# A hybrid attention and RWKV-7 layer on one core: buffers of the NSA product, gates and two key pieces moved, the second triangular solve handed out in pairs of steps, and a TensorE residual add at the end

## The chip, the cores and the metric

The kernel runs on one core of one Trainium2 chip. The metric is the device time of one execution in microseconds; lower is better. The kernel before takes 563.45 us, the median of three runs (563.41 to 565.96). One more execution was recorded by the hardware profiler, and all rows shown here come from that one.

## What is computed

One decoder layer on 256 tokens of width 2048, all in float32. Both head groups read one projection of the normalised input:

```python
h = rms_norm(x, pre_norm_g)            # (256, 2048)
feat = h @ w_in                        # q, six K/V sets, 24 gates, z_A, z_B, and r, k, v, w, a of RWKV
A = nsa_mixer(q, kc, vc, ks, vs, kw, vw, gates, ...)   # 8 heads of 128, 2 K/V groups:
                                       # compressed + selected + sliding-window attention, gated
B = rwkv7_mixer(...)                   # 16 heads of 64, a recurrence over the 256 tokens
mix = concat([A * silu(z_A), B * silu(z_B)])
out = x + rms_norm(mix @ w_out, post_norm_g)
```

The recurrence of RWKV-7 is computed in four chunks of 64 tokens, which takes triangular 32 by 32 systems, solved by substitution.

## The kernel before, in words

**Products.** A float32 operand is split into a rounded part H and a rest L, and a product is the sum of H·xH, H·xL and L·xH, so that each weight piece costs TensorE three matmuls for each 128 rows. The input projection runs over 57 pieces of 128 output features, in this order: wa (piece 0), k/r/v of the first half of the RWKV heads (1 to 12), kc, kc, vc, vc, ks, ks, kw, kw (13 to 20), k/r/v of the second half (21 to 32), q (33 to 40), z_A (41 to 48), z_B (49 to 56); the V pieces and gates, computed token-major, come ahead of piece 37. Each piece has two halves of 8 K-tiles; the weights of piece j, half h are called `hfjh` and `lfjh` (`hf191`: H of piece 19, second half), those of the output product `ho`, `lo`. SP loads a half into one of four raw buffers, ScalarE makes H (L309), VectorE makes L (L310). TensorE adds a piece up in one of two PSUM buffers of `ppool`, and VectorE empties it in `evacuate` (L594, from piece 35 on L596 and L597). Before a piece can start, the piece two ahead of it must have been emptied.

**Beside the projection** stand generators that issue a few instructions and yield: the RWKV blocks, `solve(hb)` for each half of the heads, `compress` (with weights `cw` that SP loads into the arena, L1008), and eight `nsa_head`s. Small operands of attention and the chain go through PSUM buffers called `banks`. A Python planner with estimated due times picks which one goes on, and a scheduler of the Tile framework then sets the order of each engine's instructions. On the chip each engine runs its instructions strictly in that order, and a wait for one holds all that stand behind it.

**The solve.** `us` carries the systems from the tile GR over DRAM into the arena (L799, L805). Then 31 steps of two VectorE operations each (L812, L814) follow, and the generator yields after each step. A copy (L817), a round trip over DRAM in two orders (`zt`, L820 and L829; `zs`, L821 and L838), two rounds of 32-column matmuls, and a chain over four chunks come behind it. In each step of the chain TensorE multiplies VS by KT and GR (64 by 64), VectorE empties the results (L908, L925, L935), and the next step needs them.

**Buffers.** The arena has 51 units of 128 by 256 floats, handed out and given back in program order. `xs0` and `xs1` (tags X0 and X1) hold the split input. The product of attention and gate, `mixA`, is split into 16 tiles (hi and lo; L1190 on ScalarE, L1191 on VectorE) in X1's buffer, which is read until the last half of the projection, `hf560`/`lf560`. `ks` and `kw` are emptied into an arena unit, from which L1281 and L1282 make KCH and KCL. Each z piece takes an arena unit until it has been used.

**The end.** The output product runs in four column parts of 512, for two blocks i of 128 tokens. The last three weight groups of the fourth part are done for i = 0 first. Then `finish` takes the root mean square, multiplies by `post_norm_g` (L1374), scales and adds x (L1372 on VectorE, for 512 columns L1375 on ScalarE and L1376 on GpSimd), and stores.

## Time and profile before

| | us |
|---|---|
| median of three runs | 563.45 |
| the profiled execution, its own time | 563.78 |
| its span in the trace | 562.0 |
| TensorE busy in it | 543.9 |
| VectorE busy | 436.2 |
| ScalarE busy | 320.0 |
| GpSimd busy | 58.8 |

The span is what the trace covers; 1.78 us of the profiled execution's time lie outside it. TensorE's busy time says how much of the span its matmuls fill, not how fast they were: a matmul record's end is modelled, and a record that runs at half clock is twice as long. So idle time of TensorE and its granted clock have to be read together, and a wait is best measured from the start of one group of matmuls to the start of the next, against the same group elsewhere.

### The profile page before, as it was taken

Reading aid. Unit: us, or ns where it says so; the run is one execution under the profiler, and the core shown is the slowest. Engines: PE = TensorE matmul, PEld = TensorE weight load, DVE = VectorE, ACT = ScalarE, POOL = GpSimd, SP = SyncE. Lnnn points to the kernel's source line nnn. Section 1 sums busy time; section 2 is a strip of 40 time slices with the busy share of each in tenths; the row PEclk is TensorE's granted clock in tenths of the full one; section 3 lists DMA queues with packets and bytes.
Section 4 is the critical chain, followed back from the end, with each engine's and each line's share of the span. In section 5 each row is a group of like instructions: output and inputs, shape, how many; then the busy total and the mean of one; then the engine's idle time right before and its main releaser. Section 6 shows DMA issues by size and latency. Waiting matters only on the chain. (4 is left out here: it accounts for less than half of the span.)

```text
span 562.0 us, 11515 instructions
## 1 busy us (share of the span) xinstructions
PE 543.9 (97%) x4444; PEld 496.4 (88%) x4444; DVE 436.2 (78%) x911; ACT 320.0 (57%) x592; POOL 58.8 (10%) x95
## 2 busy tenths in 40 slices
PE   9999999998799999999999999999999989999994
PEld 9999999997799999998998888888888877888883
DVE  6878997974799977678699969998757556756655
ACT  6958854743235543446767677776654345745532
POOL 3201310420000000001306100100000010000002
PEclk9999999999699999999999999999999999999997
DMA  8957455477554585643445353444644435867624
GB/s 295 377 193 263 144 177 170 151 239 217 188 188 168 172 245 185 199 152 119 138 152 188 126 147 128 162 162 141 197 150 155 152 109 184 304 187 218 194 76 150
DMA packets 41459, 102.02 MB, mean 182 GB/s; under 512 B 14235, under 2 KB 16956, under 8 KB 40764
## 3 DMA queue, kind: packets, MB, share of 16 engines
q1 hardware_dynamic: 41116, 100.98, 54.2%
q8 instruction: 35, 0.57, 0.4%
q10 hardware_dynamic: 288, 0.31, 0.2%
q14 instruction: 20, 0.16, 0.1%
HBM read 96.03 MB, written 5.24 MB: 180 GB/s over the span
## 5 line engine op out<-in xcount | busy, mean ns | idle before, releaser
L158 PE MATMUL banks<-arena 128*32 128x128 f32 (+3 forms) x470 | 30.0, 254 | 3.5 <-DMA arena<-in_cw_dram 2.5
L158 PEld LDWEIGHTS banks<-arena 128*32 128x32 f32 (+3 forms) x470 | 25.7, 137 | 7.8 <-DMA arena<-in_cw_dram 2.7
L812 DVE TENSOR_TENSOR arena<-arena 64x31 f32<-64x31 f32 (+15 forms) x62 | 20.4, 328 | 9.6 <-DMA arena<-us 5.1
L611 ACT ACTIVATE small<-small 128x256 f32<-128x256 f32 x25 | 12.4, 502 | 15.2 <-DVE small L594 15.2
L814 DVE TENSOR_TENSOR arena<-arena 64x31 f32<-64x31 f32 (+15 forms) x62 | 20.3, 328 | 0.6
L187 PE MATMUL banks<-small,arena 128*128 128x128 f32 x96 | 15.4, 273 | 0.6 <-DVE arena L1142 0.6
L699 POOL TENSOR_SCALAR arena<-arena,small 128x256 f32<-128x256 f32 x8 | 11.3, 1417 | 38.6 <-ACT arena L697 38.1
L666 DVE RECIPROCAL arena<-arena 128x256 f32<-128x256 f32 x8 | 13.8, 1738 | 1.6 <-ACT arena L663 1.6
L934 POOL MEMSET arena<- 64x256 f32 x12 | 3.7, 308 | 103.4 <-DMA zs<-arena 43.8
L1121 ACT ACTIVATE arena<-arena,mx 128x128 f32<-128x128 f32 (+1 forms) x32 | 14.1, 442 | 0.0
L612 DVE SCALAR_TENSOR_TENSOR arena<-small 128x256 f32<-128x256 f32 x25 | 11.6, 471 | 2.5 <-ACT small L611 2.5
L696 POOL TENSOR_SCALAR arena<-arena 128x256 f32<-128x256 f32 x8 | 9.3, 1158 | 38.2 <-ACT arena L695 38.2
L187 PEld LDWEIGHTS banks<-small,arena 128*128 128x128 f32 x96 | 11.5, 140 | 1.9 <-DVE arena L1142 0.9
L1376 POOL TENSOR_TENSOR y<-y,xres 128x512 f32<-128x512 f32 x2 | 2.9, 1454 | 94.2 <-ACT y L1375 94.2
L908 DVE COPY VS<-banks 64x512 f32<-64x512 f32 x8 | 5.5, 688 | 8.2 <-PE banks L158 8.1
L762 DVE TENSOR_TENSOR GR<-banks,small 128x1024 f32<-128x1024 f32 x8 | 9.7, 1211 | 2.3 <-PE banks L158 2.2
L158 PE MATMUL banks<-VS,GR 128*64 128x64 f32 x256 | 11.4, 228 | 0.0
L158 PEld LDWEIGHTS banks<-VS,GR 128*64 128x64 f32 x256 | 9.6, 137 | 1.8 <-issue 1.2
L1179 ACT ACTIVATE arena<-arena 128x256 f32<-128x256 f32 x16 | 6.6, 411 | 8.2 <-DVE arena L597 3.9
L594 DVE SCALAR_TENSOR_TENSOR small<-banks,small 128x256 f32<-128x256 f32 x25 | 10.2, 416 | 0.1
L597 DVE SCALAR_TENSOR_TENSOR arena<-banks,small 128x256 f32<-128x256 f32 x22 | 9.1, 414 | 1.1 <-PE banks L158 0.9
L1117 DVE CUSTOM_DVE_ANT_0 arena<-banks,arena 128x128 f32<-128x128 f32 (+1 forms) x32 | 9.9, 344 | 0.0
(1123 smaller groups left out, 1807.9 us busy)
## 6 DMA issues: line engine op xcount, KB each, us to landing
arena<-in_cw_dram SPq DMA_DIRECT2D x8, 512.0 KB, 5.3
arena<-in_wfm_dram SPq DMA_DIRECT2D x4, 512.0 KB, 7.9
arena<-in_xT_dram SPq DMA_DIRECT2D x2, 1024.0 KB, 5.9
xres<-in_xtok_dram SPq DMA_DIRECT2D x2, 1024.0 KB, 8.0
xr<-in_xT_dram SPq DMA_DIRECT2D x3, 512.0 KB, 7.3
bscr<-arena SPq DMA_DIRECT2D x1, 1536.0 KB, 5.9
out_dram<-y SPq DMA_DIRECT2D x5, 256.0 KB, 2.2
arena<-bscr SPq DMA_DIRECT2D x8, 128.0 KB, 3.0
```

Of the source, the lines that this page charges most:

```text
L158: last[0] = PE.matmul(o, lhsT, rhs, **kw)
L187: PE.transpose(out=o, in_=i, identity=idn)
L594: DVE.scalar_tensor_tensor(o, pt[:, :T], scale, rbc, op0=ALU.mult, op1=ALU.mult)
L611: ACT.activation(tm, f[:, 0:T], AF.Copy, scale=vcol(V_MU, c))
L612: DVE.scalar_tensor_tensor(o, f[:, 1:T + 1], omu[:, c:c + 1], tm, op0=ALU.mult, op1=ALU.add)
L666: pace(DVE.reciprocal(A.nrm[i + j], A.nrm[i + j]))
L699: POOL.tensor_scalar(fk[:], ta[:], ka2[:, m:m + 1], ka1[:, m:m + 1], op0=ALU.mult, op1=ALU.add)
L762: DVE.tensor_tensor(A.GR[:, i].rearrange("p h c t -> p (h c) t"), gp.ap.rearrange("p h (c t) -> p (h c) t", c=4), gmask[:, None, :].to_bro ...
L812: DVE.tensor_tensor(t_, U[:, 0:j, j:j + 1].to_broadcast([64, j, w]), Z[:, j:j + 1, j:32].to_broadcast([64, j, w]), op=ALU.mult)
L814: DVE.tensor_tensor(Z[:, 0:j, j:32], Z[:, 0:j, j:32], t_, op=ALU.add)
L1117: DVE.tensor_tensor_reduce(out=dst, in0=src, in1=bb, scale=1.0, scalar=-3.0e38, op0=ALU.add, op1=ALU.max, accum_out=mx[:, i, j:j + 1])
L1121: ACT.activation(dst, dst, AF.Exp, bias=mx[:, i, j:j + 1], accum_out=sm[:, i, j:j + 1])
```

## The change

The edits are these six.

1. `mixA` leaves X1: its hi tiles go into the buffers of KCH and KCL, its lo tiles into that of the lora weights (`lorS`). X1 holds instead the L weights of the last four groups of the output product (three before, in `waS` and `lorS`).
2. Twelve of sixteen z pieces leave the arena: the eight of z_A share `lorS` with what comes later, four of z_B sit in `waS`.
3. `ks` and `kw` are emptied into one of the two `fbuf` buffers that the shifted pieces use, no longer into an arena unit.
4. The second solve yields after every two steps.
5. The first quarter of the first four pieces has a fixed order on TensorE.
6. In `finish` the multiplication by `post_norm_g` moves ahead into `out_evac`; GpSimd's add and ScalarE's scaling go. VectorE scales and adds in pieces of 512 columns. For i = 1, one piece of 512 is done by TensorE: the identity times x (plain float32) plus diag(r) times y, which ScalarE copies out of PSUM and stores.

```diff
-NLAST = 3
+NLAST = 4
...
+class Kept:
+    def __init__(self, ap):
+        self.ap = ap
+
+    def __getitem__(self, i):
+        return self.ap[i]
+
+    def free(self, after=0.0):
+        pass
...
-        for q in range(2):
+        calls = []
+        for j, pt in enumerate(first):
+            for g in ((0, 1), (2, 3)) if j == 0 else ((0, 1, 2, 3),):
+                for w, x in ((Hs, xH), (Ls, xH), (Hs, xL)) if j == 0 else ((Hs, xH), (Hs, xL), (Ls, xH)):
+                    for k in g:
+                        calls.append((pt[:, :T], w[j][:, k, :], x[k],
+                                      dict(start=w is Hs and x is xH and k == 0, stop=False)))
+        mms(calls, "proj")
+        marks += [last[0]] * N_FIRST
+        for q in range(1, 2):
             for j, pt in enumerate(first):
-                for g in ((0, 1), (2, 3)) if q == j == 0 else ((0, 1, 2, 3),):
+                for g in ((0, 1, 2, 3),):
                     for k in g:
                         kk_ = 4 * q + k
                         mm(pt[:, :T], Hs[j][:, kk_, :], xH[kk_], start=kk_ == 0, stop=False)
...
-            yield ZLAT
+            if hb == 0 or j % 2:
+                yield ZLAT
...
-    KCH = rp.tile([P, 2, 528], F32R, name="KCH")
-    KCL = rp.tile([P, 2, 528], F32R, name="KCL")
+    KCH = rp.tile([P, 2, 528], F32R, tag="KCH", name="KCH")
+    KCL = rp.tile([P, 2, 528], F32R, tag="KCL", name="KCL")
...
         elif nm in ("ks", "kw"):
-            kt = pick(arena, 1)
+            kt = fbuf[turn[0] % 2][:, 1:T + 1]
             with at("evac"):
-                evacuate(kt[:], pt, j)
+                evacuate(kt, pt, j)
             for o, w in ((slice(0, 128), slice(0, 128)), (slice(400, 528), slice(128, 256))) if nm == "ks" else (
                     (slice(144, 400), slice(0, 256)),):
                 ACT.activation(KCH[:, i, o], kt[:, w], AF.Copy)
                 DVE.tensor_tensor(KCL[:, i, o], kt[:, w], KCH[:, i, o].bitcast(F32), op=ALU.subtract)
-            kt.free(2.0)
...
-            z = pick(arena, 1)
+            if i == 0:
+                zt_ = rp.tile([P, 8 if nm == "za" else 4, T], F32, tag="lorS" if nm == "za" else "waS", name="all" + nm)
+            if nm == "za" or i < 4:
+                z = Kept(zt_[:, i, :])
+            else:
+                z = pick(arena, 1)
             with at("evac"):
                 evacuate(z[:], pt, j, 0.5)
...
     until(lambda: not (lanes["nsa0"] or lanes["nsa1"] or lanes["gate"]))
-    late[0] = cp.tile([P, 16, T], F32R, tag="X1", name="mixA")
+    ma = [rp.tile([P, 4, T], F32R, tag=tag, name="mixA" + tag) for tag in ("KCH", "KCL")]
+    ml = rp.tile([P, 8, T], F32R, tag="lorS", name="mixAL")
+    late[0] = [ma[q // 4][:, q % 4, :] for q in range(8)] + [ml[:, q, :] for q in range(8)]
     for j in range(8):
         split(late[0], j, mix[0][:, j, :])
...
-    o1 = rp.tile([P, 2, 512], F32R, tag="waS", name="spare0")
-    o2 = rp.tile([P, 2, 2, 512], F32R, tag="lorS", name="spare1")
-    spare.update(zip(["o35_", "o36_", "o37_"], [o1, o2[:, 0], o2[:, 1]]))
+    so = cp.tile([P, NLAST, 2, 512], F32R, tag="X1", name="spares")
+    spare.update((f"o3{8 - NLAST + q}_", so[:, q]) for q in range(NLAST))
...
-        if n < 3:
-            DVE.tensor_tensor(yc, src, gpt[:, 512 * n:512 * n + 512], op=ALU.mult)
-            pt.free()
+        DVE.tensor_tensor(yc, src, gpt[:, 512 * n:512 * n + 512], op=ALU.mult)
+        pt.free()
...
-    def finish(pt, i):
+    def finish(i, end):
 
         r = ysum[:, 1, i:i + 1]
         ACT.activation(r, yss[:, i, 3:4], AF.Sqrt, bias=ysum[:, 0, i:i + 1], scale=1.0 / D)
         DVE.reciprocal(r, r)
-        yc = y2[:, i, 1536:2048]
-        for c0, c1 in ((0, 256), (256, 768), (1536, 2048), (768, 1280), (1280, 1536)):
-            cs = slice(c0, c1)
-            if c0 < 1536:
+        rows = out[i * P:(i + 1) * P]
+        if i == 1:
+            cs = slice(1024, 1536)
+            ob = pick(banks, 1)
+            dg, oc = pick(arena, 1), pick(arena, 2)
+            mm(ob[:], ident, xres[i][:, cs], start=True, stop=False)
+            behind(last[0], end)
+            ACT.activation(dg[:, 0:P], ident, AF.Copy, scale=r)
+            mm(ob[:], dg[:, 0:P], y2[:, i, cs], start=False, stop=True)
+            ACT.activation(oc[:], ob[:], AF.Copy)
+            ACT.dma_start(rows[:, cs], oc[:])
+        for c0 in (0, 512, 1536, 1024):
+            cs = slice(c0, c0 + 512)
+            if i == 0 or c0 != 1024:
                 DVE.scalar_tensor_tensor(y2[:, i, cs], y2[:, i, cs], r, xres[i][:, cs], op0=ALU.mult, op1=ALU.add)
-            else:
-                DVE.tensor_tensor(yc, pt[:], gpt[:, cs], op=ALU.mult)
-                ACT.activation(yc, yc, AF.Copy, scale=r)
-                POOL.tensor_tensor(yc, yc, xres[i][:, cs], op=ALU.add)
-                continue
-            SP.dma_start(out[i * P:(i + 1) * P, cs], y2[:, i, cs])
-        (SP, ACT)[i].dma_start(out[i * P:(i + 1) * P, 1536:2048], yc)
+                SP.dma_start(rows[:, cs], y2[:, i, cs])
...
+        end = last[0]
```

What the planner and the scheduler then make of it is read from each engine's order. Line numbers of the kernel after are about twenty higher (mm is L158 before and L169 after; L594, L310, L812, L814 and L908 become L614, L321, L832, L834 and L929).

On VectorE, where ks and kw are emptied and the first solve starts, before; L594 x2 are ks1 (piece 18) and kw0 (piece 19) together, behind the casts L310 of `lf201` and `lf210`:

```order
L310 TENSOR_TENSOR lf201__1726<-rf201__1724,hf201__1727 128x1024
L812 TENSOR_TENSOR arena_73<-arena_73 64x135
L1043 COPY arena_73<-banks_74 128x128
L1022 TENSOR_TENSOR arena_73<-arena_73,small_72 128x32x15 x2
L814 TENSOR_TENSOR arena_73<-arena_73 64x27x5
L812 TENSOR_TENSOR arena_73<-arena_73 64x156
L814 TENSOR_TENSOR arena_73<-arena_73 64x26x6
L310 TENSOR_TENSOR lf210__1769<-rf210__1767,hf210__1770 128x1024
L812 TENSOR_TENSOR arena_73<-arena_73 64x175
L594 SCALAR_TENSOR_TENSOR arena_73<-banks_74,small_72 128x256 x2
```

and after, the same stretch from a little earlier on:

```order
L832 TENSOR_TENSOR arena_73<-arena_73 64x31
L834 TENSOR_TENSOR arena_73<-arena_73 64x31
L832 TENSOR_TENSOR arena_73<-arena_73 64x60
L321 TENSOR_TENSOR lf200__1686<-rf200__1684,hf200__1687 128x1024
L614 SCALAR_TENSOR_TENSOR small_72<-banks_74,small_72 128x256
L834 TENSOR_TENSOR arena_73<-arena_73 64x30x2
L832 TENSOR_TENSOR arena_73<-arena_73 64x87
L834 TENSOR_TENSOR arena_73<-arena_73 64x29x3
L832 TENSOR_TENSOR arena_73<-arena_73 64x112
L321 TENSOR_TENSOR lf201__1726<-rf201__1724,hf201__1727 128x1024
```

The emptying of ks1 (L614) now stands alone right behind the cast of `lf200`, two casts earlier; that of kw0 stays behind the cast of `lf210`.

On TensorE, the last chunk steps of the second solve, before; they stand at the end of the projection, and the output product `ho00` with `mixA` follows:

```order
L158 MATMUL banks_74<-xs1_76,lf561__5321 128x256
L158 MATMUL banks_74<-arena_73 64x64 x8
L158 MATMUL banks_74<-xs1_76,lf561__5321 128x256 x7
L158 MATMUL banks_74<-VS1_3271,KT1_3272 64x64 x8
L158 MATMUL banks_74<-VS1_3271,GR1_3270 64x64 x8
L158 MATMUL banks_74<-arena_73,AR1_3269 64x128 x4
L158 MATMUL banks_74<-VS1_3271,GR1_3270 64x64 x8
L158 MATMUL banks_74<-arena_73,AR1_3269 64x128 x4
L158 MATMUL banks_74<-ho00__5373,mixA_5492 128x512 x4
```

and after, a comparable pair of chunk steps:

```order
L169 MATMUL banks_74<-xs1_76,hf531__5268 128x512 x7
L169 MATMUL banks_74<-VS1_3271,KT1_3272 64x64 x8
L169 MATMUL banks_74<-VS1_3271,GR1_3270 64x64 x8
L169 MATMUL banks_74<-arena_73,AR1_3269 64x128 x4
L169 MATMUL banks_74<-xs1_76,hf531__5268 128x512
L169 MATMUL banks_74<-xs1_76,lf531__5267 128x256 x8
L169 MATMUL banks_74<-xs0_75,hf540__5301 128x512 x3
L169 MATMUL banks_74<-VS1_3271,GR1_3270 64x64 x8
L169 MATMUL banks_74<-arena_73,AR1_3269 64x128 x4
```

Between a step's first matmuls (VS with KT and GR) and those of the next stand projection matmuls now, and these steps have moved up by several pieces. On VectorE, the split of `mixA` (L1191) stood as one block ahead of the copy that a chunk step waits for (L908), before:

```order
L310 TENSOR_TENSOR lo00__5372<-ro00__5370,ho00__5373 128x1024
L310 TENSOR_TENSOR lo01__5409<-ro01__5407,ho01__5410 128x1024
L1191 TENSOR_TENSOR mixA_5492<-arena_73,mixA_5492 128x256 x8
L908 COPY VS1_3271<-banks_74 64x4x128
L310 TENSOR_TENSOR lo02__5442<-ro02__5440,ho02__5443 128x1024
```

and after, it stands in parts, behind that copy (L929):

```order
L321 TENSOR_TENSOR lf551__5390<-rf551__5388,hf551__5391 128x1024
L929 COPY VS1_3271<-banks_74 64x4x128
L1206 TENSOR_TENSOR arena_73<-arena_73,allza_4205 128x256
L321 TENSOR_TENSOR lf560__5420<-rf560__5418,hf560__5421 128x1024
L1212 TENSOR_TENSOR mixAL_5548<-arena_73,mixAKCH_5546 128x256
L617 SCALAR_TENSOR_TENSOR arena_73<-banks_74,small_72 128x256
L1212 TENSOR_TENSOR mixAL_5548<-arena_73,mixAKCH_5546 128x256 x3
L1212 TENSOR_TENSOR mixAL_5548<-arena_73,mixAKCL_5547 128x256 x4
```

On TensorE, the first matmuls of the second solve that read the round trip (`arena,GR1`, 32 by 32), before, in the middle of piece 52:

```order
L158 MATMUL banks_74<-xs1_76,hf511__4930 128x512 x2
L158 MATMUL banks_74<-xs1_76,lf511__4929 128x256 x8
L158 MATMUL banks_74<-xs0_75,hf520__4964 128x512 x8
L158 MATMUL banks_74<-xs0_75,lf520__4963 128x256 x4
L158 MATMUL banks_74<-arena_73,GR1_3270 32x32 x32
L158 MATMUL banks_74<-xs0_75,lf520__4963 128x256 x4
L158 MATMUL banks_74<-xs1_76,hf521__4995 128x512 x8
```

and after:

```order
L169 MATMUL banks_74<-xs1_76,hf491__4895 128x512 x3
L169 MATMUL banks_74<-xs1_76,lf491__4894 128x256 x6
L198 MATMUL banks_74<-small_72,lcs5_4447 80x128 x2
L169 MATMUL banks_74<-xs1_76,lf491__4894 128x256 x2
L169 MATMUL banks_74<-arena_73,GR1_3270 32x32 x32
L169 MATMUL banks_74<-arena_73 128x256
```

They stand behind the last matmul of piece 49 now, about five halves of a piece earlier.

## Rows read from the trace of the kernel before

**Rows 1.** The page of the profile: the span, and from its first part TensorE's busy time, share and instructions.

```profile
span 562.0 us, 11515 instructions
PE 543.9 (97%) x4444; PEld 496.4 (88%) x4444; DVE 436.2 (78%) x911; ACT 320.0 (57%) x592; POOL 58.8 (10%) x95
```

**Rows 2.** The waits of TensorE over the whole span: what was waited for, us in total, times, longest us.

```profile
PE banks L158 <- DVE arena L594: 2.8, 1, 2.8
PE banks L158 <- DMA arena<-in_cw_dram: 2.5, 1, 2.5
PE banks L158 <- DVE VS L908: 1.4, 2, 1.0
...
PE banks L158 <- DVE arena L935: 0.5, 1, 0.5
PE banks L158 <- DVE arena L597: 0.5, 2, 0.2
```

**Rows 3.** Stretches of the span by engine: the stretch, its length, then busy us (and instructions) of PE, PEld, DVE, ACT and POOL, then TensorE's granted clock (1.00 is full speed), DMA share and GB/s. The start, two short stretches around the stall at 144, one in which VectorE is full, and the one with the chunk steps of the second solve.

```profile
0.00:20.00 20.00, 18.91 (x134) 18.67 (x135) 14.28 (x30) 13.94 (x26) 7.25 (x19) 1.00 0.91 331
...
139.50:143.00 3.50, 3.50 (x26) 3.25 (x16) 3.36 (x10) 0.00 (x0) 0.22 (x1) 0.51 0.61 181
...
146.30:153.20 6.90, 6.17 (x29) 6.20 (x30) 4.04 (x14) 1.99 (x5) 0.00 (x0) 0.51 0.46 152
...
340.00:360.00 20.00, 20.00 (x130) 18.08 (x129) 19.85 (x83) 15.90 (x45) 1.51 (x4) 1.00 0.51 172
...
440.00:460.00 20.00, 18.28 (x204) 15.13 (x203) 13.93 (x24) 9.79 (x21) 1.55 (x2) 1.00 0.41 138
```

**Rows 4.** The timeline of TensorE from 132 to 152: start us, us, engine, line, operation, output <- inputs, count, and in brackets the idle time before and who ended it.

```profile
132.92 2.08 PE L158 MATMUL banks<-xs,hf__1606 128*128 128x256 f32 x16
...
138.65 1.17 PE L158 MATMUL banks<-arena 128*32 128x128 f32 x32 [2.46 <-DMA arena<-in_cw_dram]
...
143.88 0.31 PE L158 MATMUL banks<-small,arena 128*128 128x32 f32 x2
147.03 3.76 PE L158 MATMUL banks<-xs,hf__1687 128*128 128x256 f32 x16 [2.84 <-DVE arena L594]
150.58 1.91 PE L158 MATMUL banks<-xs,lf__1686 128*128 128x256 f32 x8
```

**Rows 5.** The timeline of SP's queue (the issue of transfers) in the same place, the load of the first solve's data.

```profile
131.24 0.50 SPq L805 DMA_DIRECT2D arena<-us  x1
```

**Rows 6.** The timeline of VectorE in the same place.

```profile
137.78 0.20 DVE L812 TENSOR_TENSOR arena<-arena 64x31 f32<-64x31 f32 x1 [5.11 <-DMA arena<-us]
...
146.47 0.74 DVE L594 SCALAR_TENSOR_TENSOR arena<-banks,small 128x256 f32<-128x256 f32 x2
```

**Rows 7.** The timeline of TensorE from 453 to 459, the chunk steps of the second solve (inputs VS, GR, KT, AR).

```profile
453.46 1.09 PE L158 MATMUL banks<-xs,lf__5321 128*128 128x256 f32 x7
455.57 0.69 PE L158 MATMUL banks<-VS,KT 128*64 128x64 f32 x16 [1.02 <-DVE VS L908]
456.09 0.69 PE L158 MATMUL banks<-VS,GR 128*64 128x64 f32 x16
456.55 0.66 PE L158 MATMUL banks<-arena,AR 128*64 128x128 f32 x8
457.04 0.73 PE L158 MATMUL banks<-VS,GR 128*64 128x64 f32 x16
458.26 0.66 PE L158 MATMUL banks<-arena,AR 128*64 128x128 f32 x8 [0.48 <-DVE arena L935]
```

**Rows 8.** The timeline of VectorE in the same place.

```profile
452.16 2.76 DVE L1191 TENSOR_TENSOR mixA<-arena,mixA 128x256 fp32r<-128x256 f32 x8
454.84 0.67 DVE L908 COPY VS<-banks 64x512 f32<-64x512 f32 x1
```

**Rows 9.** The round trip through DRAM after the first solve: the copy on VectorE, the issues on SP, the first TensorE work that reads the result.

```profile
198.88 1.11 DVE L817 COPY arena<-arena 64x1024 f32<-64x1024 f32 x1
...
200.02 0.45 SPq L820 DMA_DIRECT2D zt<-arena  x1
...
204.47 0.98 SPq L829 DMA_DIRECT2D arena<-zt  x2
...
208.59 0.75 PE L158 MATMUL banks<-arena,GR 32*32 32x32 f32 x64
```

**Rows 10.** The timeline of all engines after the last matmul of the product.

```profile
554.70 0.69 DVE L1374 TENSOR_TENSOR y<-banks,gpt 128x512 f32<-128x512 f32 x1
...
555.31 0.15 DVE L1367 RECIPROCAL small<-small 128x1 f32<-128x1 f32 x1
555.50 3.21 DVE L1372 SCALAR_TENSOR_TENSOR y<-y,small,xres 128x256 f32<-128x256 f32 x4
...
556.30 1.47 POOL L1376 TENSOR_TENSOR y<-y,xres 128x512 f32<-128x512 f32 x1 [2.58 <-ACT y L1375]
557.80 0.36 ACTq L1379 DMA_DIRECT2D out_dram<-y  x1
```

**Rows 11.** The store's line alone from 554 on: the time from issue to landing.

```profile
DMA to landing us min/median/max: 1.9/2.2/2.4
```

**Rows 12.** From TensorE's groups of instructions by line and shape, the widest matmul of the trace whose operands are plain float32: busy us and mean ns of one record, two records to a matmul.

```profile
L158 PE MATMUL banks<-arena 128*128 128x256 f32 x32 | 9.5, 379 | 0.0
```

**Rows 13.** The timeline of VectorE where the second solve starts.

```profile
331.54 0.20 DVE L812 TENSOR_TENSOR arena<-arena 64x31 f32<-64x31 f32 x1 [3.90 <-PE banks L158]
```

More of the change, by code (lines that the diff above doesn't have):

```diff
@@ L175, in behind, with mms @@
         return ins
[L177 removed]
+    def mms(calls, name="chain"):
         prev = None
[L180 removed]
+        with at(name):
             for o, lhsT, rhs, kw in calls:
@@ L1195, in gate_b @@
         if 1 not in late:
-            late[1] = rp.tile([P, 16, T], F32R, tag="GR", name="mixB")
+            mb = rp.tile([P, 16, T], F32R, tag="GR", name="mixB")
+            late[1] = [mb[:, q, :] for q in range(16)]
         m = mix[1][:, j, :]
@@ L1311, in out_mms @@
             kk_ = 2 * (j % 4) + k
-            mm(pt, hl[:, kk_, xs], H[:, k, :], start=first and k == 0, stop=False)
-            mm(pt, hl[:, 8 + kk_, xs], H[:, k, :], start=False, stop=False)
+            mm(pt, hl[kk_][:, xs], H[:, k, :], start=first and k == 0, stop=False)
+            mm(pt, hl[8 + kk_][:, xs], H[:, k, :], start=False, stop=False)
         for k in range(2):
-            mm(pt, hl[:, 2 * (j % 4) + k, xs], L[:, k, :], start=False, stop=last and k == 1)
+            mm(pt, hl[2 * (j % 4) + k][:, xs], L[:, k, :], start=False, stop=last and k == 1)
     def out_part(n, js, pool, order=None):
@@ L1394, in hybrid_block @@
         with at("evac"):
-            finish(pts[i], i)
+            finish(i, end)
 def _bucket(n):
```

9 lines of the change are left out of this document (4 added, 5 removed).

## The prediction

> **What bounds the kernel now.** I read the page first: TensorE is busy for 543.9 of 562.0 us [rows 1]. So nearly all of the time is the products themselves, and this change removes none of them (it adds two matmuls at the end). What it can give or take is time in which TensorE stands, time in which it runs at half clock, and the tail behind the last matmul. The list of TensorE's waits is short [rows 2]: 2.8 us for one VectorE evacuation (L594), 2.5 us for a load of the compression weights, then several waits of 1.0 us and less on the chunk steps of the second solve (L908, L935, L597). The stretches by clock [rows 3] show what the list doesn't: behind the two large waits the granted clock was 0.51, from 139.5 to 143.0 and from 146.3 to 153.2. That is the 1.2 GHz level; elsewhere, up to the tail, it is 1.00. So a wait of 2.8 us cost about twice its length.
>
> **The change part by part**, against the profiled execution's 563.78 us (its span plus 1.78 us outside it), which lies 0.33 us above the median of the runs.
>
> *ks and kw in fbuf.* TensorE's start-to-start time across the stall is 147.03 − 143.88 = 3.15 us for two small matmuls that need 0.1 [rows 4], so 3.05 us. The reason is on VectorE: it stood for 5.11 us for the us load, which was issued at 131.24 [rows 5], and started on the solve and the casts at 137.78; the evacuations of ks1 and kw0 stood behind all that and came at 146.47 [rows 6]. TensorE needed the bank of ks1 at 143.9, and kw0's only 5.9 us later (two halves of a piece at about 2.9 us, as 132.92 and the next rows have it). In the order after, ks1's evacuation comes behind three solve operations and one cast. From 137.78 on that is 3 × 0.2 and 1.2, so about 140.0, 3.9 us ahead of the need. kw0's keeps its place, about 147.4 by the durations in front of it, 2.4 us ahead of its need at 149.8. So this stall goes: **−3.05**. Its half clock goes with it: the work from 147.03 to 153.2 took 6.2 us at 0.51 and would take half that at 1.00 [rows 3, 4]. The half hf200 shows it alone: 3.76 us, where hf190 took 2.08. **−3.0**. If the clock comes back less fully, this is the term that shrinks (bounds 0 to −3.1). What is late next here is the cw load at 138.65 [rows 4]: TensorE's order in front of it and its issue on SP are as before, so its 2.5 us and the 3.5 us at 0.51 behind it (1.7 us lost) stay in the sum.
>
> *mixA out of X1.* Before, the split could not be written until xs1 had been read, so its eight pieces on VectorE came in one block of 2.76 us at 452.16, ahead of the copy L908 (454.84), for which TensorE waited [rows 7, 8]. And the chunk steps stood back to back. Start to start, 453.46 to 455.57 is 2.11 us where seven matmuls at 0.12 need 0.86: 1.25 lost. 457.04 to 458.26 is 1.22 against 0.46 for the same 16 matmuls at 456.09: 0.76 lost. The listed waits for these two are 1.02 and 0.48, so start to start costs 1.3 to 1.4 times what is listed. For all the small waits on L908, L935 and L597 the list has 1.4 + 0.5 + 0.5 = 2.4 us [rows 2], so 2.4 (as listed) to 3.4. In the order after, one or more groups of projection matmuls stand between the steps, and the copies no longer stand behind the split. I take **−3.3**, the upper part, because both causes go.
>
> *z pieces, Kept, spares.* They free twelve arena units late in the kernel. No TensorE wait is listed for that [rows 2]; what it does is let the planner move the second solve up, which is in the term above. Nothing by itself: the ScalarE and VectorE operations per piece are the same.
>
> *Second solve in pairs, and earlier.* The same 62 operations, in groups of four. The matmuls that read the round trip stand behind lf491 now. In the first solve the copy ended at 199.99, zt was written at 200.02 and read at 204.47, and the first matmul came at 208.59: 8.6 us behind the copy, with TensorE busy in between, so the trip itself takes no more than that there [rows 9]. The order after leaves three to four halves of a piece, 8.6 to 11.5 us. A transfer queued behind a weight load on SP would make up to some 2.7 us of wait: 0 to +2.7, near the low end since the first solve fitted. I take **+0.6**. The cw load that is now issued one weight load later can cost from nothing to as much as the first (2.5) [rows 2]: **+0.2**.
>
> *First quarter in a fixed order.* TensorE's idle time in the first 20 us is 1.09 [rows 3], nearly all of it ahead of its first matmul, which the change doesn't touch. Bounds −0.5 to +0.3, a few matmuls of 0.12 either way; I take **0**.
>
> *Tail.* Before, VectorE's scale-and-add runs from 555.50 for 3.21 us in four pieces, while GpSimd's add at 556.30 takes 1.47 [rows 10]; the last store then lands 1.9 to 2.4 us behind its issue [rows 11]. After, the multiplication (554.70, 0.69) and the reciprocal (555.31) stay, then three pieces of 512 at no more than 0.69 each: end at 557.6 instead of 558.7, **−1.1** if this path ends last. The other path: diag(r) on ScalarE (some 0.3), a float32 matmul of 512 columns, the copy out (0.6 to 0.7) and a store issue of 0.36. The nearest matmul row has 256 columns with 0.379 us a record and two records to a matmul [rows 12]; twice that width is 0.8 us pipelined at full clock and 1.7 us at half. That puts its store's issue at 557.3 to 558.2, against 557.8 for ScalarE's store before [rows 10] and 558.8 for the last on SP. So −0.3 to −1.1: **−0.7**.
>
> *Sum:* 563.78 − 3.05 − 3.0 − 3.3 + 0.6 + 0.2 − 0.7 = **554.5 us**. With every gain at its small end (no clock back, −2.4, −0.3) and both waits in full it is 563.2; with all at the large end (−3.1, −3.4, −1.1, and −0.5 at the start), no wait new, 552.6.
>
> **A rule weighed.** The stretch with the chunk steps (440 to 460, several waits of up to 1.0 us) kept a granted clock of 1.00 [rows 3], while both waits over 2.4 us lost it. The Trainium skill (TensorE: Matmul & The Clock Gate, "A second HAM failure mode: psum-queue depth-cycling") says that frequent short idle times between groups of matmuls can make the clock fall back again and again. By that rule any new short wait would cost more than itself, some 1.7 us each if it loses what the wait at 138.65 lost, and the sum would be 556.2 with one such; the row speaks against it.
>
> **The rivals.** *B, the wait moves.* kw0's evacuation has only 2.4 us in hand, and a DMA that lands late or a cast that waits would use them up: TensorE stands later, with half clock again. The 3.05 go and come back in part, or the clock term stays: about +3, **557.5**. For it: VectorE's queue is served in order and its backlog is the same. *C, the round trip.* The second solve's first matmuls wait the full 2.7 us and lose 1.7 us of clock as behind the cw wait: 554.5 − 0.6 + 4.4 = **558.3**. For it: they moved up by five halves. Against: the first solve's trip fitted in 8.6 us. *D, the cw stall goes too*, since SP's issue order around it shifts a little: −2.5 and −1.7, **550.3**. Against: nothing ahead of it on TensorE changed. *N, the change doesn't do what it says*: the stall and the small waits come back in other places, and only the tail is left: **562 to 564**. *E, slower.* VectorE has no slack behind 340: 19.85 of 20 us busy up to 360 [rows 3]. In the second solve it stood 3.90 us at its first step [rows 13] without a TensorE wait. Its data are stored and loaded behind one more weight load now. Every us that it stands longer is a us by which all later casts and evacuations are late, and pairs of steps put four operations between casts where there were two. If it stands 6 us longer than before, beyond what four raw buffers and three L buffers cover, TensorE waits for most of it, twice, with half clock behind both (2 × (4 + 1.7) = 11.4): **566**. It decides from about 5 us on; against it, 3.90 were covered.
>
> **How the numbers follow.** Forecast 0.48, B 0.16, C 0.11, D 0.10, N 0.07, E 0.08. Likeliest: 554.5. A range of 550.5 to 560.0 takes in the forecast with its bounds, B and C and part of D, and leaves out N, E and the rest of D, some 0.18. A measurement of this kernel can tell about 0.5% (2.8 us) from no change. Faster by over that: forecast, B, C, D, and a little of N, 0.86; within it, the rest of N and a mild E, 0.07; slower, E, 0.07.
>
> **What the profile after would show.** No wait for L614 near 144, a granted clock of 1.00 from about 143 on, and the half hf200 at 2.1 us instead of 3.76; the cw wait near 138 still there, with a half clock behind it. No wait on L929 or L956 from 440 on. The mixA splits ahead of the last projection half. VectorE's last scale-and-add over by about 548.5, some 9 us earlier than before, with pieces of 0.7 us. It would be wrong if new waits stand between 280 and 440, if the half clock appears where it was not, or if the wait behind lf491 exceeds 1 us.

## The result, and the profile after

The kernel after takes 558.93 us, the median of four executions (558.42 to 559.87); the kernel before takes 563.43 beside it. The ratio is 0.9916, with an interval of 0.9886 to 0.9945: faster by 4.5 us, where 9.3 were forecast. The profiled spans are 562.0 and 556.7 us.

TensorE's waits in the kernel after, in total, times and longest, are these; they answer to [rows 2].

```profile
PE banks L169 <- DMA arena<-in_cw_dram: 1.8, 2, 1.5
PE banks L169 <- ACT arena L1402: 1.1, 1, 1.1
PE banks L169 <- POOL arena L302: 1.1, 1, 1.1
PE banks L169 <- DVE arena L1002: 1.0, 1, 1.0
PE banks L198 <- DVE arena L989: 0.7, 1, 0.7
PE banks L198 <- DVE arena L1163: 0.6, 1, 0.6
PE banks L169 <- DMA arena<-zt: 0.6, 1, 0.6
PE banks L169 <- ACT KT L755: 0.5, 1, 0.5
PE banks L169 <- DVE lf__3716 L321: 0.5, 1, 0.5
PE banks L169 <- DVE small L614: 0.5, 1, 0.5
PE banks L198 <- DVE GR L782: 0.5, 1, 0.5
```

The 2.8 us for an evacuation and the 2.4 on the chunk steps are gone. Six waits of 0.5 to 1.0 us are new (L1002, L989, zt, KT, lf__3716, and L614, another evacuation). None is large, and together they are 3.8 us. (L1402 stands in the tail; the waits for POOL, L1163 and L782 were there before, under other line numbers.)

TensorE's timeline where the two large waits stood (start, us, operation), to be read beside [rows 4]:

```profile
137.34 1.08 PE L169 MATMUL banks<-arena 128*32 128x128 f32 x32 [1.49 <-DMA arena<-in_cw_dram]
138.35 1.94 PE L169 MATMUL banks<-xs,hf__1650 128*128 128x256 f32 x14
...
141.09 0.64 PE L169 MATMUL banks<-xs,hf__1687 128*128 128x256 f32 x4
...
141.83 1.68 PE L169 MATMUL banks<-xs,hf__1687 128*128 128x256 f32 x12
...
147.19 1.72 PE L169 MATMUL banks<-xs,hf__1770 128*128 128x256 f32 x13
```

There is no stall at 144, and no half clock: the half hf200 (hf__1687) takes 2.26 us from 141.09 to 143.35, with two small matmuls in it, where it took 3.76. The clock behind the cw wait is full as well, which the forecast had not counted on; that wait is 1.49 us instead of 2.46. VectorE's timeline shows why the stall went (the last column is the idle time before the row):

```profile
136.47 0.20 DVE L832 TENSOR_TENSOR arena<-arena 64x31 f32<-64x31 f32 x1 [4.15 <-DMA arena<-us]
...
138.21 0.41 DVE L614 SCALAR_TENSOR_TENSOR small<-banks,small 128x256 f32<-128x256 f32 x1
...
145.16 0.41 DVE L614 SCALAR_TENSOR_TENSOR small<-banks,small 128x256 f32<-128x256 f32 x1
```

The evacuation of ks1 comes at 138.21, behind three solve operations and a cast, as worked out (140.0 was forecast, and the us load is 1.3 us earlier here). That of kw0 ends at 145.57, 1.6 us ahead of its need at 147.19 (2.4 were forecast). So VectorE's own standing for the us load, [rows 6], is still there and now costs TensorE nothing.

Where the time came from and went is easiest seen in a balance. For each matmul record I took the time from its start to the next start, less what this form usually takes over all the runs, and added that up by stretch. What is left is waiting, half clock and the cost of changing between small groups; below zero means better than usual. In us:

| stretch | before | after | difference |
|---|---|---|---|
| 0 to 20 | 2.2 | 1.9 | −0.4 |
| 20 to 120 | −0.9 | −1.0 | −0.1 |
| 120 to 160 | 9.95 | 1.7 | −8.3 |
| 160 to 240 | 0.3 | 2.0 | +1.7 |
| 240 to 340 | 3.2 | 3.9 | +0.7 |
| 340 to 480 | 1.2 | 2.1 | +0.95 |
| 480 to the last product matmul | −0.7 | −0.3 | +0.4 |

The differences add up to about −5, and the last group of product matmuls starts 4.8 us earlier (553.33 before, 548.53 after). The tail from that group's end to the span's end went from 8.05 to 7.55. So in these two executions 8.3 us were won in one place, and nearly half of it was lost in four others. Two cautions belong to the table. With the usual time taken as a median or a trimmed mean, by shape alone or by shape and neighbour, a stretch's difference moves by some 0.3 to 0.6 us. And it is one execution on each side: a3_tail below, which runs the code of the kernel before up to the tail, has 7.9 from 120 to 160 and not 9.95, so that the same stretch gives 6.2 against that one.

Two of the new waits, on VectorE and TensorE near 210, in their timelines:

```profile
207.10 0.75 PE L169 MATMUL banks<-arena,GR 32*32 32x32 f32 x64 [0.55 <-DMA arena<-zt]
...
218.71 0.47 PE L169 MATMUL banks<-xs,hf__2580 128*128 128x256 f32 x2 [0.48 <-DVE small L614]
```

```profile
213.71 3.26 DVE L527 SCALAR_TENSOR_TENSOR arena<-arena,small 128x256 f32<-128x256 f32 x8 [4.28 <-DMA arena<-in_xT_dram]
...
218.13 0.43 DVE L614 SCALAR_TENSOR_TENSOR small<-banks,small 128x256 f32<-128x256 f32 x1
```

The first solve's copy starts at 196.53 and takes 1.12, and TensorE gets zt at 207.10: 9.45 us behind the copy, where [rows 9] had 8.6 without a wait. Without its wait of 0.55 it would have come 8.9 us behind the copy, so against the copy TensorE is not early here: the round trip itself took longer than before. Why it did is not shown (after_third and a7_x1 below come 8.8 us behind the copy and do not wait). The evacuation at 218.13 stands behind a block of 3.26 us that itself had waited 4.28 us for its load of x. Before, that block began at 216.89:

```profile
216.89 3.26 DVE L507 SCALAR_TENSOR_TENSOR arena<-arena,small 128x256 f32<-128x256 f32 x8 [2.70 <-DMA arena<-in_xT_dram]
```

It comes 3.2 us sooner now, while TensorE's work at this place comes 8.4 us sooner (the half hf__2549 starts at 215.19 instead of 223.55). Here TensorE is early, and the load has not kept up.

Then the second half of the heads. ScalarE, VectorE and TensorE at the norm behind the last chunk step:

```profile
469.64 1.09 ACT L1361 ACTIVATE y<-banks 128x512 f32<-128x512 f32 x2 [1.24 <-PE banks L169]
470.75 1.28 ACT L987 ACT_TABLE_LOAD   x1
```

```profile
472.38 0.25 DVE L988 RECIPROCAL small<-small 128x16 f32<-128x16 f32 x1 [1.00 <-ACT small L987]
472.67 1.23 DVE L989 TENSOR_TENSOR arena<-arena,small 128x1024 f32<-128x1024 f32 x1
```

```profile
473.95 0.66 PE L198 MATMUL banks<-small,arena 128*128 128x128 f32 x4 [0.66 <-DVE arena L989]
...
477.21 0.50 PE L169 MATMUL banks<-ho__5591,mixAKCH 128*128 128x512 f32 x1 [0.97 <-DVE arena L1002]
```

The square root needs another activation table, whose load takes 1.28 us and starts only when ScalarE has copied two product parts, for which it had waited 1.24 us; VectorE stands 1.00 us for it and TensorE 0.66 us for VectorE. Then a product group waits 0.97 us for a PSUM buffer that L1002 must empty.

The tail after, TensorE, then VectorE, then ScalarE, beside [rows 10]:

```profile
548.53 0.62 PE L169 MATMUL banks<-spares,mixB 128*128 128x512 f32 x2
548.99 1.02 PE L169 MATMUL banks<-xres,small 128*128 128x512 f32 x2
551.16 1.12 PE L169 MATMUL banks<-y,arena 128*128 128x512 f32 x2 [1.15 <-ACT arena L1402]
```

```profile
550.71 2.08 DVE L1409 SCALAR_TENSOR_TENSOR y<-y,small,xres 128x512 f32<-128x512 f32 x3
```

```profile
552.32 0.60 ACT L1404 ACTIVATE arena<-banks 128x512 f32<-128x512 f32 x1 [1.22 <-PE banks L169]
552.95 0.35 ACTq L1405 DMA_DIRECT2D out_dram<-arena  x1
```

VectorE's three pieces take 2.08 us together. Before, the last store was SP's, issued at 558.76, 5.4 us behind the start of the last product group (553.33). Now the last one is ScalarE's at 552.95, 4.4 us behind it (548.53): 1.0 us sooner. But the span's end is only 0.5 us sooner behind that group. The rest is the landing: ScalarE's store takes 2.8 us from issue to landing, where SP's took 2.4 at most [rows 11].

```profile
DMA to landing us min/median/max: 2.8/2.8/2.8
```

### The profile page after: what moved, and what is told of

It reads as the page before. It is cut to its first block, busy times and chain, and to the rows that moved or that the text cites. A ratio compares the mean times of both kernels' runs of the same rounds, so it can differ in the third digit from the quotient of the medians.

```text
span 556.7 us, 11510 instructions
## 1 busy us (share of the span) xinstructions
PE 542.6 (97%) x4448; PEld 492.7 (88%) x4448; DVE 434.2 (78%) x910; ACT 319.5 (57%) x592; POOL 54.9 (10%) x93
## 4 chain that ended last, share of the span: by engine, by line
PE 84%; DVE 6%; DMA 5%; ACT 2%; issue 1%; SPq 1%; DVEq 0%; ACTq 0%
PE banks L169 82%; DMA arena<-in_cw_dram 2%; PE banks L198 2%; DMA zs<-arena 1%; DMA xr<-in_xT_dram 1%; DMA us<-GR 1%; DMA arena<-zt 1%; DVE GR L782 1%; DVE arena L1002 0%; DVE arena L527 0%; DVE arena L834 0%; DVE arena L832 0%; ACT arena L1142 0%; ACT L987 0%; ACT L715 0%
## 5 line engine op out<-in xcount | busy, mean ns | idle before, releaser
L169 PE MATMUL banks<-arena 128*32 128x128 f32 (+3 forms) x470 | 29.5, 253 | 3.2 <-DMA arena<-in_cw_dram 1.8
L169 PEld LDWEIGHTS banks<-arena 128*32 128x32 f32 (+3 forms) x470 | 25.0, 136 | 7.2 <-DMA arena<-in_cw_dram 2.2
L832 DVE TENSOR_TENSOR arena<-arena 64x31 f32<-64x31 f32 (+15 forms) x62 | 20.4, 329 | 6.2 <-DMA arena<-us 5.6
L834 DVE TENSOR_TENSOR arena<-arena 64x31 f32<-64x31 f32 (+15 forms) x62 | 20.4, 330 | 0.7
L719 POOL TENSOR_SCALAR arena<-arena,small 128x256 f32<-128x256 f32 x8 | 9.3, 1164 | 39.3 <-ACT arena L717 39.1
L614 DVE SCALAR_TENSOR_TENSOR small<-banks,small 128x256 f32<-128x256 f32 x29 | 11.9, 417 | 0.1
L169 PEld LDWEIGHTS banks<-VS,GR 128*64 128x64 f32 x256 | 9.6, 137 | 2.5 <-issue 1.4
L955 POOL MEMSET arena<- 64x256 f32 x12 | 3.7, 307 | 81.2 <-DVE lf__2469 L321 44.8
L782 DVE TENSOR_TENSOR GR<-banks,small 128x1024 f32<-128x1024 f32 x8 | 9.7, 1215 | 2.3 <-PE banks L169 2.2
L169 PE MATMUL banks<-VS,GR 128*64 128x64 f32 x256 | 11.4, 228 | 0.0
L743 POOL COPY AR<-arena 128x4 f32<-128x4 f32 x8 | 7.3, 909 | 34.9 <-DVE arena L733 34.9
L169 PE MATMUL banks<-AR,arena 64*128 64x128 f32 x128 | 10.0, 287 | 0.0
L716 POOL TENSOR_SCALAR arena<-arena 128x256 f32<-128x256 f32 x8 | 8.1, 1018 | 17.5 <-ACT arena L715 17.5
L527 DVE SCALAR_TENSOR_TENSOR arena<-arena,small 128x256 f32<-128x256 f32 x16 | 6.5, 479 | 4.3 <-DMA arena<-in_xT_dram 4.3
L169 PEld LDWEIGHTS banks<-AR,arena 64*128 64x128 f32 x128 | 8.1, 187 | 1.4 <-issue 0.3
```

The costliest lines, as they stand in the source:

```text
L169: last[0] = PE.matmul(o, lhsT, rhs, **kw)
L614: DVE.scalar_tensor_tensor(o, pt[:, :T], scale, rbc, op0=ALU.mult, op1=ALU.mult)
L719: POOL.tensor_scalar(fk[:], ta[:], ka2[:, m:m + 1], ka1[:, m:m + 1], op0=ALU.mult, op1=ALU.add)
L782: DVE.tensor_tensor(A.GR[:, i].rearrange("p h c t -> p (h c) t"), gp.ap.rearrange("p h (c t) -> p (h c) t", c=4), gmask[:, None, :].to_bro ...
L832: DVE.tensor_tensor(t_, U[:, 0:j, j:j + 1].to_broadcast([64, j, w]), Z[:, j:j + 1, j:32].to_broadcast([64, j, w]), op=ALU.mult)
L834: DVE.tensor_tensor(Z[:, 0:j, j:32], Z[:, 0:j, j:32], t_, op=ALU.add)
```

## The experiments

Each run stood beside the kernel before on the same chip. The executions of one kernel spread over 1.5 to 6.6 us here, and the intervals reach 0.2 to 0.3% to either side. For what is smaller, and for where it lies, I use the balance of the one profiled execution of each, as above:

| run | median (before) | ratio, interval | 120–160 | 160–240 | 240–340 | 340–480 |
|---|---|---|---|---|---|---|
| before (profiled) | | | 9.95 | 0.3 | 3.2 | 1.2 |
| after | 558.93 (563.43) | 0.9916, 0.9886–0.9945 | 1.7 | 2.0 | 3.9 | 2.1 |
| after_again | 559.46 (564.12) | 0.9919, 0.9898–0.9941 | 1.7 | 1.6 | 3.9 | 1.8 |
| after_third | 559.72 (563.44) | 0.9927, 0.9903–0.9951 | 2.5 | 1.6 | 5.4 | 1.9 |
| a1_ks | 560.70 (564.12) | 0.9943, 0.9925–0.9961 | 1.9 | 1.7 | 3.9 | 2.0 |
| a5_arena | 562.06 (562.98) | 0.9987, 0.9967–1.0007 | 7.8 | 0.2 | 3.7 | 0.3 |
| a2_mixz | 564.20 (562.98) | 1.0019, 0.9999–1.0038 | 8.6 | 0.6 | 3.3 | 2.0 |
| a4_each | 560.16 (562.98) | 0.9943, 0.9913–0.9973 | 1.8 | 2.7 | 3.8 | 2.0 |
| a7_x1 | 558.45 (562.98) | 0.9917, 0.9890–0.9945 | 1.5 | 2.4 | 3.9 | 0.3 |
| a3_tail | 562.98 (564.12) | 0.9988, 0.9967–1.0009 | 7.9 | 0.9 | 3.5 | 1.2 |
| c_table | 559.84 (564.12) | 0.9933, 0.9909–0.9957 | 1.4 | 2.3 | 5.5 | 0.8 |
| f3_late_x | 571.26 (563.44) | 1.0134, 1.0113–1.0155 | 1.6 | 1.1 | 15.1 | 1.1 |
| g_nolow | 564.18 (563.44) | 1.0009, 0.9981–1.0038 | 1.7 | 2.5 | 5.6 | 1.7 |

**ks and kw alone**: the kernel before with this one edit.

```diff
-            kt = pick(arena, 1)
+            kt = fbuf[turn[0] % 2][:, 1:T + 1]
...
-                evacuate(kt[:], pt, j)
+                evacuate(kt, pt, j)
...
-            kt.free(2.0)
```

> The kernel before with ks and kw emptied into fbuf, and nothing else of the change. Theory: this edit alone removes the stall at 144 with its half clock, and the reordering that it sets off brings little: minus 6 to minus 8 us, 555.5 to 557.5, faster than the kernel after. Rival: the new short waits between 160 and 400 (about 2.5 us in the kernel after) come with this edit too: minus 3 to minus 5, 558.5 to 560.5.

It gains 3.4 us at the median, near the second of the two expectations. The balance shows −8.0 from 120 to 160, nearly all of what the full change wins there, and +1.4, +0.7 and +0.8 in the three stretches behind. So the give-back from 160 to 240 comes with this edit alone. From 240 to 340 the case is weaker: a3_tail, with the old code there, stands 0.3 above the kernel before, and a5_arena below, without this edit, has 3.7. Its list of waits has the wait for zt already, and the old chunk steps besides:

```profile
PE banks L158 <- DVE VS L908: 1.7, 2, 1.3
...
PE banks L158 <- DMA arena<-zt: 0.7, 1, 0.7
```

**The change without ks and kw**: the reverse of the same edit, made to the kernel after.

> The kernel after with ks and kw emptied into an arena unit again, all else of the change kept. Theory: the stall at 144 and its half clock are back, and the new short waits between 160 and 340 are gone: 2.5 to 4 us slower than the kernel after. Rival: the stall was removed by the other edits (arena units free earlier) as well: within 1 us of the kernel after.

The stall is back, 4.1 us now where the kernel before had 2.8, with half clock behind it (hf__1687 takes 3.55 us):

```profile
146.40 3.55 PE L169 MATMUL banks<-xs,hf__1687 128*128 128x256 f32 x16 [4.05 <-DVE arena L614]
```

The stretch from 160 to 240 is at 0.2 again, with no wait for zt. All other edits together come to 0.9 us at the median, with an interval that takes in zero, and that is with a stall 1.2 us longer. The two runs agree from both sides: the gain is ks and kw, and the loss from 160 to 240 comes with it. That TensorE's being early is the reason is shown at 218 alone.

**mixA and the z pieces alone** (with the fixed first quarter): the kernel after with ks and kw in the arena, the old tail, and a yield after each step.

```diff
-            if hb == 0 or j % 2:
-                yield ZLAT
+            yield ZLAT
...
```

> The kernel after with ks/kw back in the arena, the second solve yielding after every step and the old tail: what is left of the change is mixA in KCH, KCL and lorS, the z pieces out of the arena and the fixed order at the start. Theory: the waits on the chunk steps (3.3 us start to start) go, but others of 2 to 3 us come in their place between 400 and 480, above all at the norm of the second half; the stall at 144 stays: 0.3 to 1.5 us faster than before. Rival (the prediction's term): all of the 3.3 us is gained.

Nothing is won, where 0.3 to 1.5 us had been expected. TensorE still waits for the chunk steps:

```profile
PE banks L169 <- DVE VS L928: 0.9, 1, 0.9
PE banks L169 <- ACT arena L918: 0.8, 1, 0.8
```

So taking the mixA split out of the way does not remove them. The median does not price mixA by itself: the stall for ks1 is 4.05 us here, 2.84 in the kernel before, and the clock fell once more behind the chunk waits (0.70 from 464 to 468).

**No pairs**: the kernel after with that yield alone undone.

> The kernel after with the second solve yielding after every step, as before. Theory: the pairs are what moves the second solve and its chain up, which brought nothing by itself: within 1 us of the kernel after. Rival: without the pairs the solve ends later, the chain lies back to back again and 2 us or more are lost.

The chunk waits return (L928 0.9, L918 0.8, L955 0.4), so it is the pairs that remove them. But 340 to 480 stands at 2.0 with them and at 2.1 without: the norm's waits (L989, L1002) aren't in its list. One sort of wait was exchanged for another, though not quite evenly: this profile's 2.0 holds a lost clock as well (0.57 from 460 to 464).

**mixA back in X1**: the kernel after, with the spares where mixA was.

```diff
-    ma = [rp.tile([P, 4, T], F32R, tag=tag, name="mixA" + tag) for tag in ("KCH", "KCL")]
-    ml = rp.tile([P, 8, T], F32R, tag="lorS", name="mixAL")
+    mx1 = cp.tile([P, 16, T], F32R, tag="X1", name="mixA")
...
-    so = cp.tile([P, NLAST, 2, 512], F32R, tag="X1", name="spares")
+    so = [rp.tile([P, 2, 512], F32R, tag=tag, name="sp" + tag) for tag in ("KCH", "KCL")]
+    s2 = rp.tile([P, 2, 2, 512], F32R, tag="lorS", name="splorS")
...
```

> The kernel after with mixA back in X1 (all 16 tiles) and the L weights of the last four groups in KCH, KCL and lorS. Theory: the chunk steps wait for VectorE again, but the norm of the second half comes later and does not; within 1 us of the kernel after. Rival (the prediction's term): 3.3 us slower than the kernel after.

It is as fast as the kernel after (558.45, the same ratio). Its chunk waits stay away, though they had been expected back, and 340 to 480 is at 0.3. Moving mixA, the edit to which the forecast gave 3.3 us, can be taken back at no cost. The wait at the PSUM buffer stays:

```profile
PE banks L169 <- DVE arena L1002: 1.0, 1, 1.0
```

All eight profiles in which the second solve goes in pairs have this wait, wherever mixA lies, and none of the five others: it came with the pairs. The wait for L989 is in the kernel after, its two repeats and g_nolow, and neither here nor in a4_each nor in a5_arena: it took the pairs, the moved mixA and the early ks and kw together.

**The tail alone**, in the kernel before (the diff of `finish` above).

> The kernel before with the change's tail alone (TensorE adds x to one piece, GpSimd's add gone, pieces of 512). Theory: the tail is worth 0.5 us, as the two spans have it: 562.9. The prediction's term was 0.7 with 0.3 to 1.1 as bounds: 562.7. Rival: the path over TensorE's idle, half-clocked matmul ends later than the old one: 563.4 or more.

The ratio cannot tell it from nothing (0.9988, −0.33% to +0.09%). In the profile it has the same wait of 1.1 us of TensorE for diag(r). From the last product group (552.36) to the span's end at 560.6 it takes 8.2 us, against 8.7 before: −0.4. It is also a second execution of the old code up to there. Behind the stall for ks1, again of 2.8 us, its clock is back to full by 150, where the kernel before kept 0.51 to 153.2 [rows 3]:

```profile
146.00:150.00 4.00, 3.43 (x17) 3.46 (x18) 3.21 (x13) 0.94 (x4) 0.00 (x0) 0.57 0.63 204
150.00:154.00 4.00, 4.00 (x36) 4.00 (x35) 2.80 (x7) 2.19 (x4) 0.00 (x0) 1.00 0.29 105
```

**The table loaded sooner**: the kernel after with a small Sqrt right behind the square.

```diff
+        if hb == 1:
+            ACT.activation(warm, rns[:, 0:2], AF.Sqrt)
```

> The kernel after, with one small square root more on ScalarE behind the square of the second half's norm, so that the table for square roots is loaded before two copies that wait for TensorE, and not behind them. Theory: TensorE's waits near 473 and 477 (0.66 and 0.97 us) come from the table load of 1.28 us that stands between the square and the reciprocal; moved ahead it gives back 1 to 2 us: 557 to 558. Rival: the waits come from VectorE's queue and the shared PSUM bank; the time stays within 0.3 us of the kernel after.

The load moves ahead of the copies and L989's wait is gone (340 to 480 at 0.8); the 1.0 us at the PSUM buffer stays. VectorE and TensorE have the same order there as in the kernel after, so the table is the cause of that one wait. The median doesn't resolve it.

**The block for x behind the evacuation**: a7_x1 with the order of two VectorE groups fixed (`ev` holds the evacuation issued last).

```diff
...
-            yield 4.0
+            yield 9.0
...
-                DVE.scalar_tensor_tensor(xv[:, k, :], xv[:, k, :], vcol(V_G, 8 * q + k), rbc, op0=ALU.mult,
-                                         op1=ALU.mult)
+                behind(DVE.scalar_tensor_tensor(xv[:, k, :], xv[:, k, :], vcol(V_G, 8 * q + k), rbc, op0=ALU.mult,
+                                                op1=ALU.mult), ev[0])
...
-            DVE.scalar_tensor_tensor(o, pt[:, :T], scale, rbc, op0=ALU.mult, op1=ALU.mult)
+            ev[0] = DVE.scalar_tensor_tensor(o, pt[:, :T], scale, rbc, op0=ALU.mult, op1=ALU.mult)
```

> As a7_x1, and the eight VectorE operations that renew the input for the second projection layout are ordered behind the evacuation that stood behind them (they wait for a load of x that lands no earlier than before). Theory: the wait for that evacuation near 218 (0.5 to 1.7 us in the profiles so far) goes and nothing else moves: 0.5 to 1.5 us faster than a7_x1, 557 to 558 where the kernel after takes 559, and less than 0.3 us left of the wait at 218. Rival: the renewed input is late instead, and TensorE waits for it near 230: no gain.

This is 7.8 us slower than the kernel before and 11.5 slower than the kernel after on the same chip (559.72); a7_x1 itself ran on another. The block leaves its old place and comes at 244.75, where a chunk step's copy stands behind it. VectorE and TensorE there:

```profile
244.75 3.25 DVE L528 SCALAR_TENSOR_TENSOR arena<-arena,small 128x256 f32<-128x256 f32 x8
248.04 0.69 DVE L930 COPY VS<-banks 64x512 f32<-64x512 f32 x1
```

```profile
248.78 1.12 PE L169 MATMUL banks<-VS,KT 128*64 128x64 f32 x16 [3.25 <-DVE VS L930]
```

Behind that, the renewed input is late (waits of 1.2 and 2.1 us for `hr` up to 275, and 3.2 up to 340), and the clock falls at three of these places (0.57 from 248 to 252, 0.62 from 276 to 280, 0.63 from 341 to 345). The wait near 218 went, as expected, and the gain did not come: 0.3 to 1.6 us there was the cheap place for the block. The longer yield is part of the edit, so the order alone is not priced.

**VectorE relieved**: the kernel after without the L casts of pieces 25 to 40. It leaves out the product L·xH of these pieces: the matmuls run, but read H.

```diff
+        if name in NOLOW:
+            H = wp.tile(shape, F32R, tag="wh", name="h" + name, bufs=4)
+            ACT.activation(H, raw, AF.Copy)
+            return H, H
```

> The kernel after without the L weights of pieces 25 to 40: their L·xH matmuls read H, so that VectorE casts no L there (1.2 us for each half, up to 32 halves), and TensorE does as many matmuls as before; part of the product is left out of the result's low bits. Theory: from 280 to 340 VectorE's queue, full in the kernel after, takes back part of the lead; with the casts gone the waits there (about 3.5 us over the trace's usual) fall under 1 us, and the wait at 206 for the round trip stays. Rival: those waits are latencies of chains over ScalarE, GpSimd and DMA; they stay above 2 us.

VectorE's work from 120 to 400 falls by 37 us (234.01 to 197.16 busy), and TensorE's excess from 160 to 340 rises from 5.9 to 8.1 (5.5 and 7.0 in the repeats of the kernel after). Its waits are others:

```profile
PE banks L170 <- DVE lt__3042 L326: 2.0, 1, 2.0
PE banks L199 <- ACT arena L1166: 1.9, 1, 1.9
PE banks L170 <- ACT VS L808: 1.7, 1, 1.7
```

The first is a cast behind the same block for x, which waits for its load; the others are ScalarE. The edit moves the order of everything, so it is no clean test. But the idea that VectorE's amount of work sets the waits up to 340 finds no support: with 16% less of it there is no less waiting.

**The same kernel again**, twice.

> The kernel after, unchanged, once more. Theory: its times lie between 558.4 and 559.9 because the wait for the compression weights near 136 differs from one execution to the next; where it lasts 1.5 us the granted clock stays 1.00 (558.4 to 558.6), where it lasts 2.5 us or more a stretch at 0.51 follows and costs 1 to 2 us more. Rival: that wait is always the same and the spread comes from elsewhere; then the profile shows the same 1.5 us and a clock of 1.00 whatever the time.

> The kernel after, unchanged, beside the others of this call, to compare them with on one chip: 558.5 to 560 by both theories.

Three medians of one kernel, 558.93, 559.46 and 559.72, put the gain at 3.7 to 4.7 us. The profiled execution of after_again (559.42) has a cw wait of 1.56 us with the clock at 1.00, as the kernel after (558.53) had, so that wait is not what sets these two apart. The start alone varies (1.9, 3.3 and 2.2 us up to 20), and the third shows something else, at 320. The windows of the kernel after, then of its third run (TensorE's granted clock is the number behind the POOL column):

```profile
320.00:322.00 2.00, 1.54 (x13) 1.38 (x13) 1.64 (x6) 1.04 (x4) 0.00 (x0) 1.00 0.48 143
322.00:324.00 2.00, 2.00 (x12) 1.72 (x11) 0.00 (x0) 1.55 (x5) 0.00 (x0) 1.00 0.58 96
```

```profile
320.00:322.00 2.00, 1.24 (x8) 0.93 (x8) 2.00 (x5) 1.05 (x4) 0.00 (x0) 0.90 0.63 242
322.00:324.00 2.00, 2.00 (x9) 1.81 (x8) 0.25 (x2) 1.99 (x6) 0.00 (x0) 0.50 0.76 128
```

And TensorE's timeline of the third run in this place:

```profile
319.79 0.33 PE L198 MATMUL banks<-small,arena 128*128 128x128 f32 x1 [0.64 <-DVE arena L1163]
320.42 0.31 PE L198 MATMUL banks<-small,lcs 128*80 128x128 f32 x1 [0.31 <-ACT cTt L1174]
321.19 1.20 PE L198 MATMUL banks<-small,arena 128*128 128x128 f32 x6 [0.46 <-DVE GR L782]
...
322.89 3.07 PE L169 MATMUL banks<-xs,hf__3861 128*128 128x512 f32 x8
```

The kernel after has the same three waits, of the same length, and keeps 1.00; its hf__3861 takes 2.07 us. In the third run the clock is at its lower level behind them and the same eight matmuls take 3.07; the whole place costs 1.6 us more. c_table shows the same loss there (0.58 from 322 to 326), after_again and a7_x1 don't.

## Why the prediction was right, and where not

Right on the sign and in the range, 4.4 us too low at the centre. That it lies in the range is in part luck: had the cw wait and its half clock stayed as the forecast had them, the time would have been about 561.6 by estimate (558.93 + 1.0 + 1.7), outside it.

- *The ks/kw stall with its half clock, −6.05.* Right, in mechanism, place and order of the queue; a1_ks and a5_arena show it from both sides. The 3.0 for the clock was read from one execution, and a costly one: in a3_tail and a5_arena the clock is back by 150, in about half the time. The stretch gave −8.3, because the cw wait shrank by 1.0 us and its half clock of 1.7 went as well. That is 2.7 of rival D's 4.2 us. The edit to ks and kw is not needed for it: the clock fell behind the cw wait in both profiles of the old code (the kernel before, 2.46 us, and a3_tail, 1.82) and in none of the eleven others, a2_mixz and a5_arena among them (1.2 to 1.9 us, once 2.33). What made the difference is open.
- *mixA out of X1, −3.3.* This step failed, in the sentence "both causes go". The chunk waits did go, but the split in front of L908 was a neighbour, not the cause: a2_mixz moves it and keeps the waits, a7_x1 puts it back and has none. The pairs, which let the second solve run earlier, removed them and brought the 0.97 us at the PSUM buffer, and with mixA moved and ks and kw early the 0.66 for L989 as well. From 340 to 480 the balance came out at +0.95, not −3.3. Even with the pairs and without L989's wait (a5_arena, a7_x1) this stretch gains only 0.9.
- *Second solve and cw, +0.8.* The second solve's matmuls behind lf491 waited for nothing, where +0.6 was taken; the later cw load cost 0.3, near its +0.2. TensorE did wait for a round trip, but for the first solve's, which the forecast had as fitting. That a wait of the forecast kind turned up there is chance. What the sum put at nothing is what 8 us of lead do to TensorE's later waits: +1.7 from 160 to 240, of which the waits for zt, cw and the evacuation at 218 are 1.3, and +0.7 up to 340. This is the second miss, and it is N in small: part of the stall came back in other places. The last line of the prediction named the sign to look for, new waits between 280 and 440.
- *Tail, −0.7.* It came to −0.5. VectorE ended 4.3 us behind the start of the last product group (552.79 − 548.53), as worked out (557.6 − 553.33), and the store behind TensorE's piece was issued 4.4 behind it, within the bounds worked out (557.3 to 558.2). What the term had too small is that store's landing: 2.8 us, where 1.9 to 2.4 were assumed.
- *Start, 0.* It came to −0.4, within its bounds, and three runs of one kernel differ by more.
- *The rule weighed.* The text held the stretch 440 to 460 against the Trainium skill's section (TensorE: Matmul & The Clock Gate, "A second HAM failure mode: psum-queue depth-cycling"). The runs bear the rule out in part: the three waits near 320 (0.64, 0.30 and 0.46 us) were followed by a lost clock in two of the six profiles that have them (after, its two repeats, a1_ks, a7_x1, c_table), at 1.6 us, and both a4_each and a2_mixz lost it behind chunk waits of 0.4, 0.8 and 0.9 us (0.57 from 460 to 464 in the first). A single row at 1.00 could not speak against it. The 1.7 us per loss was sized well.

What stays open: why the first solve's round trip took longer, what in the order behind 240 costs the 0.7, and why the clock falls behind the same waits in one execution and not in another.

## What to carry to other kernels

A stall that is taken out of the bounding engine's path makes that engine early for what stands behind it, and a transfer or queue that had been just in time can become a short wait: count the slack of the next several, not only the next one. An operation that stands ahead of a late one on the same queue is a suspect, and no more, until it has been moved alone. Where executions differ by as much as the terms, a balance by stretch helps to tell which edit did what when medians can't; it is one execution, so the same code should be profiled twice before a term is sized from it.
